# The last quarter of a late modulation moved beside the output projection, and a bias row added later

## The chip, the cores and the metric

The kernel runs on one core of a Trainium2 chip. The metric is the device time of a whole execution in microseconds (us), the median of several runs. Five engines work side by side, each through its own queue in order: PE multiplies matrices, DVE, ACT and POOL work element by element, and SP here only issues DMAs.

## The reference, cut to what matters

One block of a diffusion backbone over 1024 latent and 256 context tokens, 1024 wide. Six rows of modulation come from the condition vector c; the last three (the shift and scale of the MLP, `sh2` and `sc2`, and its gate `gt2`, called g2 below) and the gate `gt1` (g1) are wanted late.

```python
m = jax.nn.silu(cvec) @ w_ada + b_ada
sh1, sc1, gt1, sh2, sc2, gt2 = jnp.split(m[:, None, :], 6, axis=-1)
p_lat = modulate(rmsnorm(x, g_mix), sh1, sc1) @ w_in
p_ctx = modulate(rmsnorm(ctx, g_mix), csh1, csc1) @ w_in
y_lat = token_mixers(p_ctx, p_lat, ...)      # mLSTM, Mamba-2 SSD, RG-LRU
x = x + gt1 * (y_lat @ w_out)
x = x + gt2 * (jnp.square(jax.nn.relu(modulate(rmsnorm(x, g_mlp), sh2, sc2) @ w_mlp1 + b_mlp1)) @ w_mlp2 + b_mlp2)
return rmsnorm(x, g_final)
```

Everything is float32. A product is three matmuls on operands split into a high and a low part.

## The kernel before

The work runs in stages (times are those of the profiled run). Until 70 us the input is loaded and normalised, and the modulation's first third is computed on PE. From 70 to 156 us come the gates and the first feature tile of the RG-LRU, to 235 us its second tile and the q, k and v projections with their convolutions. To 365 us the mLSTM runs backward and forward with the projections x, c and b beside it, to 447 us the z projections and the backward part of the SSD. From 447 us the SSD sweep goes over eight latent chunks of 128 tokens, and the last projections fill PE between its steps; each chunk starts with products of a selector matrix, `SELB`, and needs the state of the chunk before. By 600 us w_out is split into high and low parts, and to 662 us the output projection runs: for each of eight token tiles two groups of 24 matmuls, the gate g1, the residual, the norm, and transposes into the MLP's operand (`x2_tile`). Then come the two MLP products, each by a seven-product scheme, the first of 56 products in eight blocks to about 976 us, the second to the end.

A list scheduler sets the order ahead of time: it places instructions on each engine's queue by a priority, and `at()` gives parts of the mixers due times from a table, `PLAN`, which fills the gaps of one part with another's work.

The late modulation is the product of the condition with columns 2048 to 6143 of `w_ada`, done on DVE: 64 jobs of 128 rows by 512 columns, eight to a row of the accumulator. A job loads 256 KB into a buffer and adds it, scaled per partition, to `ACCA` (line 727; the first of eight is line 725). After eight jobs `ada_flush` sums the accumulator over the partitions with four small matmuls against ones and adds the bias into `MODL`. The jobs are strewn in by `proj`: five ahead of each projection xr, q, k, v, x, c and b, until 64 are done. The buffer is a ring of six in the first stages, later a single tile. The last flush turns all of `MODL` into rows and stores them in `GD`, from where g1 and g2 are broadcast to all partitions (`bcast_row`).

Beside the output projection POOL multiplies `b_mlp2` by g2 into two tiles `WX` (line 1212) and adds them to the finished residual tiles 0 to 4 (line 1235) before these are stored to `X2D`. The first MLP product then carries side jobs on POOL between its products: tiles 5 to 7 of `X2D` are loaded, get b2*g2 added and are stored again (line 1483), and the 32 row tiles of `w_mlp2` are multiplied by g2 and stored (line 1485). The splits of the first MLP's operands run on ACT and DVE (line 1311), the sums and differences of its scheme on DVE (line 1339).

## Time and profile before

| | us |
|---|---|
| runs | 1299.17, 1303.20, 1304.24 |
| median | 1303.2 |
| profiled execution | 1300.48 |
| its span | 1298.8 |
| busy PE / PEld / DVE | 1228.0 / 964.4 / 979.9 |
| busy ACT / POOL | 564.8 / 285.1 |
| mean granted TensorE clock | 0.986 |

A busy share is an average over all stages. The views below cut it into stretches; in the timelines the time in brackets is how long the engine had been idle, and what it waited for. PEld is the loading of weights, which runs beside the matmuls.

### The profile page before, as it was taken

The numbers are of one execution on the slowest core, as the hardware profiler recorded it, in microseconds if no ns is written. First come the engines' busy times: TensorE is split into PE (matmuls) and PEld (weight loads), VectorE is DVE, ScalarE is ACT, GpSimd is POOL, SyncE is SP. The second block draws the span as 40 slices with busy tenths as digits, with TensorE's granted clock in tenths as the row PEclk, the third lists the DMA queues.
The fourth block names the chain that finished last, engine by engine and source line by source line (L and its number), as shares of the span: only waits on it lengthen the run. The fifth ranks groups of instructions, "written<-read, shape, count | busy, mean of one in ns | idle before, by whom it ended". The sixth has DMA issues, their size and how long they took to land.

```text
span 1298.8 us, 16517 instructions
## 1 busy us (share of the span) xinstructions
PE 1228.0 (95%) x6066; PEld 964.4 (74%) x6066; DVE 979.9 (75%) x1416; ACT 564.8 (43%) x891; POOL 285.1 (22%) x290
## 2 busy tenths in 40 slices
PE   4888898999999889999999999999999999999997
PEld 1566667788786667677888888888787888888886
DVE  3798977787774675677569876677668988989985
ACT  3546572343333334254466534553357433333432
POOL 2430212212322235213500254345200000000000
PEclk9899999999999999999999999999999999999999
DMA  9444402642325522145333589877679142330112
GB/s 314 155 134 143 130 17 82 183 131 70 125 63 165 169 75 74 57 147 170 116 112 130 175 296 323 290 258 277 243 255 365 75 149 111 128 132 1 56 58 98
DMA packets 122790, 196.48 MB, mean 151 GB/s; under 512 B 11126, under 2 KB 71892, under 8 KB 121172
## 3 DMA queue, kind: packets, MB, share of 16 engines
q1 hardware_dynamic: 122708, 195.42, 45.5%
q8 instruction: 48, 0.79, 0.3%
q14 instruction: 34, 0.28, 0.1%
HBM read 140.76 MB, written 54.63 MB: 150 GB/s over the span
## 4 chain that ended last, share of the span: by engine, by line
PE 56%; DVE 3%; DMA 2%; ACT 1%; issue 1%; POOL 1%; POOLq 0%; DVEq 0%; SPq 0%; ACTq 0%
PE pp L53 28%; PE pd L53 16%; PE psx L53 6%; PE psa L53 2%; PE psb L53 2%; PE psl L53 1%; PE pst L53 1%; DMA wx<-ZD 1%; DMA rw<-in_w_mlp_dram 1%; PE pst L1266 1%; DVE rw L1339 0%; DMA g1B<-GD 0%; POOL KV L1062 0%; POOL xp L1020 0%; DVE rbd L857 0%
## 5 line engine op out<-in xcount | busy, mean ns | idle before, releaser
L53 PE MATMUL pd<-xh,wht 128*128 128x512 f32 (+1 forms) x304 | 126.2, 418 | 3.2 <-DVE wx L1111 1.7
L53 PE MATMUL pd<-xh,wlt 128*128 128x512 f32 (+1 forms) x304 | 126.3, 417 | 1.7 <-POOL wlt L352 1.7
L53 PE MATMUL pd<-xl,wht 128*128 128x512 f32 (+1 forms) x304 | 123.2, 409 | 3.9 <-DVE xl L235 1.8
L1485 POOL TENSOR_TENSOR ax<-ax,g2B 128x1024 f32<-128x1024 f32 x32 | 84.6, 2647 | 92.4 <-DMA ax<-in_w_mlp_dram 92.4
L53 PE MATMUL pp<-ob,yb 128*128 128x512 f32 x324 | 97.6, 395 | 0.0
L352 POOL TENSOR_TENSOR wlt<-wraw,wht 128x512 fp32r<-128x512 f32 x40 | 58.2, 1456 | 177.6 <-ACT wht L351 143.6
L1339 DVE TENSOR_TENSOR rw<-rw 128x1024 f32<-128x1024 f32 (+1 forms) x33 | 64.8, 1965 | 32.0 <-DMA rw<-in_w_mlp_dram 19.1
L1684 POOL TENSOR_TENSOR ss<-ss,V 128x1 f32<-128x1 f32 x8 | 5.2, 644 | 355.9 <-DVE ss L1683 355.9
L53 PEld LDWEIGHTS pp<-ob,yb 128*128 128x128 f32 x324 | 60.7, 187 | 14.9
L53 PEld LDWEIGHTS pd<-xh,wht 128*128 128x128 f32 (+1 forms) x304 | 58.0, 191 | 17.9 <-DVE wx L1111 2.1
L53 PEld LDWEIGHTS pd<-xl,wht 128*128 128x128 f32 (+1 forms) x304 | 57.9, 190 | 16.1 <-DVE xl L235 4.9
L53 PEld LDWEIGHTS pd<-xh,wlt 128*128 128x128 f32 (+1 forms) x304 | 58.0, 191 | 14.1 <-POOL wlt L352 2.5
L351 ACT ACTIVATE wht<-wraw 128x512 fp32r<-128x512 f32 (+2 forms) x50 | 28.5, 581 | 67.0 <-PE pd L53 17.4
L53 PE MATMUL pp<-ob,wht 128*128 128x512 f32 x144 | 53.5, 395 | 0.0
L1310 ACT ACTIVATE ya<-rw 128x1024 fp32r<-128x1024 f32 x26 | 27.5, 1058 | 42.0 <-issue 14.2
L1400 ACT ACTIVATE pp<-pp,V 128x512 f32<-128x512 f32 x35 | 23.0, 656 | 50.9 <-DVE pp L1395 50.7
L53 PE MATMUL psx<-xc,wht 128*128 128x256 f32 (+1 forms) x192 | 42.8, 293 | 1.4 <-POOL xc L235 0.7
L53 PE MATMUL pp<-ya,wlt 128*128 128x512 f32 x124 | 43.0, 391 | 0.0
L53 PEld LDWEIGHTS psx<-xc,wht 128*128 128x128 f32 (+1 forms) x192 | 33.7, 188 | 8.1 <-POOL xc L235 1.2
L1311 DVE TENSOR_TENSOR ya<-rw,ya 128x1024 fp32r<-128x1024 f32 x18 | 24.9, 1388 | 13.2 <-ACT ya L1310 13.1
L53 PE MATMUL pp<-yb,wlt 128*128 128x512 f32 x88 | 34.3, 390 | 0.0
L53 PE MATMUL pd<-ya,wlt 128*128 128x512 f32 x88 | 34.2, 389 | 0.0
(838 smaller groups left out, 3461.4 us busy)
## 6 DMA issues: line engine op xcount, KB each, us to landing
ax<-in_w_mlp_dram SPq DMA_DIRECT2D x33, 512.0 KB, 6.2
rw<-in_w_mlp_dram SPq DMA_DIRECT2D x32, 512.0 KB, 5.5
W2S<-ax SPq DMA_DIRECT2D x32, 512.0 KB, 3.5
wraw<-in_w_in_dram SPq DMA_DIRECT2D x44, 256.0 KB, 2.9
radt<-in_w_ada_dram SPq DMA_DIRECT2D x40, 256.0 KB, 3.0
ada<-in_w_ada_dram SPq DMA_DIRECT2D x16, 512.0 KB, 5.5
HD<-wraw SPq DMA_DIRECT2D x16, 512.0 KB, 3.7
HD<-g1B SPq DMA_DIRECT2D x16, 512.0 KB, 3.3
```

What stands on the lines that cost most here:

```text
L53: return T.matmul(o, l, r, start=start, stop=stop)
L351: S.activation(out=ph, in_=pr, func=AF.Copy)
L352: (V if split or name[0:2] == "xr" else G).tensor_tensor(out=pl, in0=pr, in1=ph.bitcast(F32), op=ALU.subtract)
L1266: T.transpose(pt[:, k, :], xn[:, (4 * g + k) * P:(4 * g + k + 1) * P], ident)
L1310: S.activation(out=hi[:, c], in_=src[:, c], func=AF.Copy)
L1311: (e or V).tensor_tensor(out=lo[:, c], in0=src[:, c], in1=hi[:, c].bitcast(F32), op=ALU.subtract)
L1339: RS[2] = (e or V).tensor_tensor(out=q[o], in0=q[x0], in1=q[x1], op=op)
L1400: S.activation(out=ps, in_=ps, func=AF.Relu, bias=V2[:, 40 + f:41 + f])
L1485: G.tensor_tensor(out=u, in0=u, in1=g, op=ALU.mult)
L1684: G.tensor_tensor(out=rs, in0=ss[:, 1:2], in1=MHALF, op=ALU.pow)
```

## The change

The 64 jobs are split differently. Ahead of the projections there are fewer now: three for xr, q, k and v, four for x, c and b, which makes 48. After the SSD's features the sixth row is flushed, and the first 8 of the 32 rows of 128 in `MODL`, which hold g1, go to `GD`. The last 16 jobs, the two accumulator rows of g2, are issued in the output projection, four after each of the first four token tiles, with a ring of four buffers in `AXA` and an accumulator in `AX2`. With the fifth tile come the last flush, the second transposition and store, the broadcast of g2 and the products b2*g2. The additions of b2*g2 before the spill are gone: all eight tiles of `X2D` get them in the first MLP product, where 40 side jobs in place of 35 start two products sooner. The splits of that product's weights whose tile shares its place with `AXA` come later. `PLAN` is as it was.

```diff
--- before.py
+++ after.py
@@ -354,17 +354,19 @@
             ls.append(wl)
         return hs, ls
 
+    NADA = {"q": 3, "k": 3, "v": 3, "x": 4, "c": 4, "b": 4, "z": 0, "g": 0, "o": 0}
+
     def proj(name, col, segs, evac, gates=False):
         m = 48 if gates else P
         early = name.startswith("xr")
         if early:
-            ada_late(5)
+            ada_late(3)
         with (prio({"xr0": pxr0, "xr1": pxr1}[name]) if early else tc.high_priority()):
             if gates:
                 hs, ls = wsplit(name, ((0, C_IG, 16), (16, C_DT, 16)), 32, True)
             else:
-                if not early and not name.startswith("z"):
-                    ada_late(5)
+                if not early:
+                    ada_late(NADA[name[0]])
                 hs, ls = wsplit(name, ((0, col, P),), P, False)
         for grp in ([(0,), (1, 2)] if len(segs) == 3 else [(0,), (1,)]):
             ps = {}
@@ -699,32 +701,31 @@
     ada_pos = [0]
     GD = drp.tile([32, P], F32, name="GD")
 
-    def ada_flush(r):
-        pm = psx[:, 0:4]
+    ACC = [ACCA]
+
+    def ada_flush(r, pm):
         for i in range(4):
-            mm(pm[:, i:i + 1], ACCA[:, i * P:(i + 1) * P], ones[:, 0:1])
-        V.tensor_tensor(out=MODL[:, 4 * r:4 * r + 4], in0=pm, in1=V2[:, 4 * r:4 * r + 4], op=ALU.add)
-
-    def ada_late(n):
+            mm(pm[:, i:i + 1], ACC[0][:, i * P:(i + 1) * P], ones[:, 0:1])
+        V.tensor_tensor(out=MODL[:, 4 * r:4 * r + 4], in0=pm[:, 0:4], in1=V2[:, 4 * r:4 * r + 4], op=ALU.add)
+
+    def mod_rows(r0, n, pm, o):
+        T.transpose(pm[0:n, 0:P], MODL[:, r0:r0 + n], ident)
+        S.activation(out=o[0:n, 0:P], in_=pm[0:n, 0:P], func=AF.Copy)
+        SY.dma_start(out=GD[r0:r0 + n], in_=o[0:n, 0:P])
+
+    def ada_late(n, ring=None):
         for _ in range(n):
             i = ada_pos[0]
             ada_pos[0] += 1
             r, k = i // KT, i % KT
-            if k == 0 and 0 < r <= 8:
-                ada_flush(r - 1)
-                if r == 8:
-                    V.scalar_tensor_tensor(out=MODL[:, 16:24], in0=MODL[:, 16:24], scalar=1.0, in1=V2[:, 32:40], op0=ALU.add, op1=ALU.mult)
-                    T.transpose(psx[0:32, 0:P], MODL, ident)
-                    S.activation(out=WX[0][0:32, 0:P], in_=psx[0:32, 0:P], func=AF.Copy)
-                    SY.dma_start(out=GD, in_=WX[0][0:32, 0:P])
-            if r >= 8:
-                return
+            if k == 0 and r in (1, 2, 3, 4, 5, 7):
+                ada_flush(r - 1, ring.get([P, 4]) if ring else psx)
             t = radt.get([P, 512])
             SY.dma_start(out=t, in_=w_ada[k * P:(k + 1) * P, 2048 + 512 * r:2560 + 512 * r])
             if k == 0:
-                V.tensor_scalar(out=ACCA, in0=t, scalar1=SCL[:, k, 0:1], scalar2=None, op0=ALU.mult)
+                V.tensor_scalar(out=ACC[0], in0=t, scalar1=SCL[:, k, 0:1], scalar2=None, op0=ALU.mult)
             else:
-                V.scalar_tensor_tensor(out=ACCA, in0=t, scalar=SCL[:, k, 0:1], in1=ACCA, op0=ALU.mult, op1=ALU.add)
+                V.scalar_tensor_tensor(out=ACC[0], in0=t, scalar=SCL[:, k, 0:1], in1=ACC[0], op0=ALU.mult, op1=ALU.add)
 
     with ExitStack() as st:
         cp = st.enter_context(pool("cp"))
@@ -1135,6 +1136,9 @@
     with at(PLAN["mo"]):
         mlstm_out()
     ssd_features()
+    ada_flush(5, psx)
+    V.scalar_tensor_tensor(out=MODL[:, 16:24], in0=MODL[:, 16:24], scalar=1.0, in1=V2[:, 32:40], op0=ALU.add, op1=ALU.mult)
+    mod_rows(0, 8, psx, WX[0])
     z_spill()
     ssd_back()
     YC = [SAt[0], SAt[1]]
@@ -1200,16 +1204,14 @@
     X2L = [p2a.tile([P, KT, 512], F32R, tag="x0l", name="x0l")]
     g1B = p2a.tile([P, D], F32, name="g1B")
     g2B = p2a.tile([P, D], F32, name="g2B")
-    OPX = p2a.tile([P, 2048], F32R, tag="ax1", name="opx")
+    AXA = p2a.tile([P, 2048], F32, tag="ax1", name="axa")
     AX2 = p2a.tile([P, 1536], F32, name="ax2")
     p2x = ExitStack()
     p2b = p2x.enter_context(tc.tile_pool(name="p2b", bufs=1, reuse_waits="tile"))
     wo_prep(5, p2b.tile([P, D], F32R, name="woh5"), p2b.tile([P, D], F32R, name="wol5"))
-    for g, r in ((g1B, 0), (g2B, 24)):
-        bcast_row(g, GD[r:r + 8, :].rearrange("r q -> (r q)"))
-    for h in range(2):
-        bcast_row(WX[h], a["b_mlp2"][0, 512 * h:512 * h + 512])
-        G.tensor_tensor(out=WX[h], in0=WX[h], in1=g2B[:, 512 * h:512 * h + 512], op=ALU.mult)
+    bcast_row(g1B, GD[0:8, :].rearrange("r q -> (r q)"))
+    ACC[0] = AX2[:, 1024:1536]
+    radt = Sub([AXA[:, 512 * i:512 * i + 512] for i in range(4)])
     pW = Sub(pA.t + pB.t + pL.t + [psx] + PD[0][:2])
 
     pso = {}
@@ -1226,13 +1228,8 @@
 
     wo_mm((0, 0), (0, 1), (1, 0), (1, 1))
     XQ, X2T = [], {}
-    LATE = 5
 
     def x2_store(t):
-        if t < LATE:
-            for h in range(2):
-                o = X2T[t][:, 512 * h:512 * h + 512]
-                G.tensor_tensor(out=o, in0=o, in1=WX[h], op=ALU.add)
         SY.dma_start(out=X2D[t], in_=X2T[t])
 
     def x2_tile(t):
@@ -1282,6 +1279,15 @@
     for t in range(6):
         x2_tile(t)
         x2_store(t)
+        if t < 4:
+            ada_late(4, pT)
+        if t == 4:
+            ada_flush(7, pT.get([P, 4]))
+            mod_rows(24, 8, pT.get([P, P]), AXA)
+            bcast_row(g2B, GD[24:32, :].rearrange("r q -> (r q)"))
+            for h in range(2):
+                bcast_row(WX[h], a["b_mlp2"][0, 512 * h:512 * h + 512])
+                G.tensor_tensor(out=WX[h], in0=WX[h], in1=g2B[:, 512 * h:512 * h + 512], op=ALU.mult)
 
 
     wox.close()
@@ -1324,6 +1330,7 @@
     XIN = {1: "11", 2: "21", 6: "T2", 5: "T1", 7: "T3", 3: "22", 4: "T4"}
     AIN = {1: "11", 2: "12", 3: "12", 4: "22", 5: "21", 6: "11", 7: "21"}
     rq = {n: RW[:, 1024 * j:1024 * j + 1024] for j, n in enumerate(("11", "12", "21", "22"))}
+    OPX = p2a.tile([P, 2048], F32R, tag="ax1", name="opx")
     R1 = [WHT, WLT]
     ops1 = []
     U1 = AX2[:, 0:1024]
@@ -1470,7 +1477,7 @@
     W2S = drp.tile([4096, D], F32, name="W2S")
     AX1 = p2a.tile([P, 2048], F32, tag="ax1", name="ax1")
     w2b = [AX1[:, 0:1024], AX1[:, 1024:2048], AX2[:, 0:1024]]
-    jobs = [(X2D[t], X2D[t], None) for t in range(LATE, 8)] + [(w2[r * P:(r + 1) * P, :], W2S[r * P:(r + 1) * P, :], g2B) for r in range(32)]
+    jobs = [(X2D[t], X2D[t], None) for t in range(8)] + [(w2[r * P:(r + 1) * P, :], W2S[r * P:(r + 1) * P, :], g2B) for r in range(32)]
 
     def side_job(r):
         if 0 <= r - 2 < len(jobs):
@@ -1494,7 +1501,7 @@
         if n > 8:
             op1(n + 4)
         with tc.issue_after(ld[0].ins):
-            side_job(n - 14)
+            side_job(n - 12)
 
 
     ORDER = (1, 2, 5, 6, 3, 7, 4)
```

On DVE, at the exponentials of the first RG-LRU feature (lines 669 to 674 before), the queue before reads as follows; `wx` is the accumulator and `radt` the ring of loaded tiles:

```order
L727 SCALAR_TENSOR_TENSOR wx_94<-radt_612,SCL,wx_94 128x512
L669 SCALAR_TENSOR_TENSOR GR<-cp_622,GR 128x1282
L727 SCALAR_TENSOR_TENSOR wx_94<-radt_613,SCL,wx_94 128x512
L670 SCALAR_TENSOR_TENSOR cp_617<-cp_617,cp_623 128x1282
L727 SCALAR_TENSOR_TENSOR wx_94<-radt_614,SCL,wx_94 128x512
L727 SCALAR_TENSOR_TENSOR wx_94<-radt_615,SCL,wx_94 128x512
L670 SCALAR_TENSOR_TENSOR cp_620<-cp_620,cp_623 128x1282
L706 TENSOR_TENSOR MODL<-psx,V_78 128x4
L725 TENSOR_SCALAR wx_94<-radt_610,SCL 128x512
L727 SCALAR_TENSOR_TENSOR wx_94<-radt_611,SCL,wx_94 128x512
L669 SCALAR_TENSOR_TENSOR cp_619<-cp_622,cp_619 128x1282
```

And in the changed kernel (its lines are one to three higher there):

```order
L728 SCALAR_TENSOR_TENSOR wx_94<-radt_612,SCL,wx_94 128x512
L672 SCALAR_TENSOR_TENSOR cp_617<-cp_617,cp_623 128x1282
L728 SCALAR_TENSOR_TENSOR wx_94<-radt_613,SCL,wx_94 128x512
L671 SCALAR_TENSOR_TENSOR GR<-cp_622,GR 128x1282
L672 SCALAR_TENSOR_TENSOR cp_620<-cp_620,cp_623 128x1282
L671 SCALAR_TENSOR_TENSOR cp_619<-cp_622,cp_619 128x1282
L676 TENSOR_TENSOR cp_617<-GR,cp_617 128x1282
L676 TENSOR_TENSOR cp_620<-cp_619,cp_620 128x1282
L680 SCALAR_TENSOR_TENSOR GR<-cp_618,cp_617 128x256
L680 SCALAR_TENSOR_TENSOR cp_619<-cp_621,cp_620 128x256
```

The feature's own steps now follow each other; the jobs that stood between them are ahead of them or gone.

On PE, ahead of the fifth chunk of the sweep, the queue before has the chunk's preparation (a transposition of `TB` and the score products of `cT` and `bT`) amid the filling projection matmuls (`pd`):

```order
L53 MATMUL pd_66<-xl_86,wht 128x512
L53 MATMUL pd_66<-xh_85,wlt 128x512
L53 MATMUL pst_561<-ones,wx_94 128x1
L849 MATMUL pst_562<-ident,TB 128x128
L53 MATMUL pst_561<-ones,wx_94 128x1 x3
L53 MATMUL psa_563<-cT,bT 128x128
L53 MATMUL psb_564<-cT,bT 128x128
L53 MATMUL pd_65<-xh_87,wht 128x512
L53 MATMUL pd_65<-xl_88,wht 128x512
```

In the changed kernel that preparation stands further ahead, and the filling matmuls run up to the chunk's own products:

```order
L53 MATMUL pd_66<-xl_86,wht 128x512
L53 MATMUL pd_66<-xh_85,wlt 128x512
L53 MATMUL pst_561<-ones,wx_94 128x1 x4
L53 MATMUL psl_565<-rbd_1677,rcol_1681 128x512
L53 MATMUL psl_565<-MK_591,identR 128x512
L53 MATMUL psx<-rbd_1677,rcol_1682 128x512
```

Between the fourth chunk's first `SELB` product and the fifth's there are 78 filling matmuls before and 110 now.

On SP, at the end of the output projection, before:

```order
L1246 DMA x_6_5040<-in_x_dram 128x1024
L1236 DMA X2D<-x_5_4928 128x1024
L1246 DMA x_7_5130<-in_x_dram 128x1024
L1336 DMA rw<-in_w_mlp_dram 128x4x256 x4
L1236 DMA X2D<-x_6_5040 128x1024
L1236 DMA X2D<-x_7_5130 128x1024
```

And now:

```order
L724 DMA axa<-in_w_ada_dram 128x512 x3
L1243 DMA x_6_5034<-in_x_dram 128x1024
L1233 DMA X2D<-x_5_4921 128x1024
L1243 DMA x_7_5124<-in_x_dram 128x1024
L714 DMA GD<-axa 8x128
L1158 DMA g2B<-GD 128x1024
L1343 DMA rw<-in_w_mlp_dram 128x4x256 x4
L1233 DMA X2D<-x_6_5034 128x1024
L1233 DMA X2D<-x_7_5124 128x1024
```

The last jobs' loads and the two transfers through `GD` stand ahead of the first weights of the MLP (`rw`).

## Rows read from the trace of the kernel before

**Rows 1.** The page's list of busy times: us, share of the span, instructions.

```profile
PE 1228.0 (95%) x6066; PEld 964.4 (74%) x6066; DVE 979.9 (75%) x1416; ACT 564.8 (43%) x891; POOL 285.1 (22%) x290
```

**Rows 2.** Windows by stage: length, busy us of PE, PEld, DVE, ACT, POOL.

```profile
70.00:156.00 86.00, 75.92 (x363) 57.05 (x363) 80.84 (x129) 44.47 (x65) 18.93 (x28) 0.98 0.47 142
156.00:235.00 79.00, 71.74 (x336) 55.57 (x338) 55.49 (x49) 42.07 (x59) 18.54 (x36) 0.96 0.23 65
235.00:365.00 130.00, 126.11 (x712) 102.73 (x711) 105.51 (x258) 48.29 (x91) 29.95 (x63) 0.97 0.41 122
447.00:545.00 98.00, 90.40 (x698) 65.70 (x696) 66.44 (x126) 33.84 (x63) 40.61 (x32) 1.00 0.24 66
600.00:662.00 62.00, 62.00 (x290) 50.69 (x289) 34.27 (x59) 26.02 (x71) 25.45 (x23) 1.00 0.35 117
```

**Rows 3.** Windows of 50 us, same columns.

```profile
600.00:650.00 50.00, 50.00 (x234) 40.91 (x233) 28.00 (x48) 20.18 (x56) 24.90 (x22) 1.00 0.39 130
...
900.00:950.00 50.00, 48.05 (x204) 38.99 (x203) 34.04 (x32) 23.06 (x34) 13.71 (x6) 0.97 0.61 218
```

**Rows 4.** Windows, DVE's work of line 727, then of line 725, alone.

```profile
70.00:156.00 86.00, 23.95 (x28) 0.98 0.47 142
...
70.00:156.00 86.00, 1.92 (x4) 0.98 0.47 142
```

**Rows 5.** Timeline of DVE: start us, us, engine, line, operation, count, idle before.

```profile
128.80 1.50 DVE L669 SCALAR_TENSOR_TENSOR GR<-cp,GR 128x1282 f32<-128x1282 f32 x1 [2.13 <-ACT cp L668]
...
152.68 2.81 DVE L682 TENSOR_TENSOR cp<-GR,cp 128x1024 f32<-128x1024 f32 x1
...
171.25 1.50 DVE L669 SCALAR_TENSOR_TENSOR GR<-cp,GR 128x1282 f32<-128x1282 f32 x1 [7.01 <-ACT cp L668]
```

**Rows 6.** Waits of PE, 156 to 235 us: total us, times, longest.

```profile
PE pst L53 <- ACT GR L661: 4.0, 1, 4.0
```

**Rows 7.** The chain that ended last: start us, us, what.

```profile
482.44 11.56 PE pd L53 x50
...
597.60 0.76 DVE xn L1259
...
644.50 5.57 PE psb L53 x24
```

**Rows 8.** Timeline of PE around one flush.

```profile
361.89 0.95 PE L53 MATMUL psx<-ones,wx 128*128 128x1 f32 x8
362.70 0.49 PE L53 MATMUL pd<-xl,wht 128*128 128x512 f32 x1
```

**Rows 9.** Line 727: ns min/median/max; then who waited for it.

```profile
L727 DVE SCALAR_TENSOR_TENSOR wx<-radt,SCL,wx x35: 721/745/1786, 80.0 to 225.8; 128x512 f32<-128x512 f32 x35
...
  PE psx L53: 4.0, 2
```

**Rows 10.** The page's DMA issues: count, KB each, us to landing.

```profile
radt<-in_w_ada_dram SPq DMA_DIRECT2D x40, 256.0 KB, 3.0
```

**Rows 11.** Timeline of SP: the first weights of the MLP.

```profile
659.33 2.03 SPq L1336 DMA_DIRECT2D rw<-in_w_mlp_dram  x4
```

**Rows 12.** Lines 1235 and 1485 on POOL: ns min/median/max.

```profile
L1235 POOL TENSOR_TENSOR x<-x,wx x10: 1280/1286/2279, 598.6 to 635.3; 128x512 f32<-128x512 f32 x10
...
L1485 POOL TENSOR_TENSOR ax<-ax,g2B x32: 2386/2408/3483, 759.7 to 931.0; 128x1024 f32<-128x1024 f32 x32
```

**Rows 13.** Timeline of DVE, the last block of the first MLP product.

```profile
921.45 1.32 DVE L1339 TENSOR_TENSOR rw<-rw 128x1024 f32<-128x1024 f32 x1 [6.57 <-DMA rw<-in_w_mlp_dram]
...
931.14 3.35 DVE L1339 TENSOR_TENSOR rw<-rw 128x1024 f32<-128x1024 f32 x1
```

**Rows 14.** Waits of PE, 662 to 960 us.

```profile
PE pp L53 <- DVE uu L1391: 2.0, 1, 2.0
```

**Rows 15.** Window between the sweep's fourth and fifth chunk, columns as in rows 2.

```profile
477.70:503.00 25.30, 24.93 (x156) 19.62 (x155) 13.88 (x24) 8.85 (x17) 11.78 (x9) 1.00 0.19 53
```

## The prediction, made before the changed kernel was run

> **What bounds the kernel now.** I read the page's list of busy times first: PE is busy for 1228.0 of 1298.8 us [rows 1], so nearly all there is to win lies in the 70 us in which it is not. Then I cut the span by stage [rows 2], because an average hides where those 70 us are. From 600 us on PE is full: 62.00 of 62 us in the output projection, and in the first MLP product the one dent is 1.95 us at 900 to 950 [rows 2, 3]. The idle time that an edit can reach is in the mixers. Of these the stage from 70 to 156 us (gate mathematics and the first RG-LRU feature) stands out: DVE is busy there for 80.84 of 86 us and PE for 75.92, so PE has 10.1 us idle and DVE 5.2. In every other mixer stage DVE stands well below PE: 55.49 of 79, 105.51 of 130, 66.44 of 98 [rows 2].
>
> Third, I looked at who fills DVE in that stage. The accumulations of the late modulation (line 727, and line 725 for the first of each eight) take 23.95 us in 28 and 1.92 us in 4: 32 of the 64 jobs, 25.9 us, stand in the one stage where DVE is short [rows 4]. DVE's timeline shows its queue without a gap over 2.13 us until the feature's last sum at 152.68 [rows 5].
>
> **The change part by part.** The profiled run took 1300.48 us, 1.7 of them outside its span; it is 2.7 us below the median of 1303.2. The sum is made on 1300.48, and 2.7 added at the end.
>
> *Sixteen jobs fewer in the mixers.* By the new order all sixteen disappear ahead of the first RG-LRU feature's end: 32 jobs stood there, now 16. From there to the sweep 32 stand in both. So the relief falls into the DVE-bound stage alone. Half of its jobs is 14 x 0.855 us (23.95 / 28) + 2 x 0.48 = 12.9 us off DVE [rows 4]. Not all of it can reach the end. Late next is ACT, whose exponentials and squares (line 668) already make DVE wait 2.13 us; the second feature, with none of these jobs in between, shows how long that wait is without cover: 7.01 us [rows 5]. I therefore take off 7.0 - 2.1 = 4.9 us and have 12.9 - 4.9 = **-8.0 us**, which also stays within PE's 10.1 us idle. Bounds: -12.9 if ACT keeps up, 0 if ACT's or PE's own chain sets the pace (ACT makes PE wait 4.0 us in the next stage, line 661 [rows 6]). A loss is excluded, as nothing is added to this stage.
>
> *Matmuls that change places.* With other work ready at other times, the scheduler puts 63 projection matmuls behind the sweep's first chunk that stood ahead of it (between the first chunk and the last 159 before, 226 now). Fifty of them run in 11.56 us [rows 7], 0.231 each: 14.6 us. They leave a stage in which PE is 97% busy (126.11 of 130) and enter one where it is 92% busy (90.40 of 98) [rows 2]. A matmul that moves from one full stretch to another changes nothing, so I take **0**, with bounds of -7.6 (the sweep's idle PE time takes half of them for nothing) and +14.6 (the stages ahead end no sooner, and the sweep is longer by all of them).
>
> *Flushes.* Two of the eight flushes, which turn an accumulated row by four small products, leave the mixers for the output projection, and a second transposition joins them. A flush holds PE for 0.81 us, from 361.89 to 362.70 [rows 8]. In the saturated stage that is 2 x 0.81 + 0.2 = 1.8 us more, in the mixers 1.6 less; I take **+0.2** (up to +1.8, if the mixers do not return it).
>
> *Sixteen jobs in the output projection.* DVE gets 14 x 0.745 (the median of line 727 [rows 9]) + 2 x 0.48 = 11.4 us. It is busy for 34.27 of 62 there; 45.7 of 62 fit beside PE's 62.00 [rows 2]. What hides them is PE's queue of 24-matmul groups of 5.57 us each [rows 7], issued two token tiles ahead. Ahead of the first normalised tile (597.60 [rows 7]) five jobs, 3.7 us, now stand where three splits of a weight operand stood, which go behind it. I take **0**: PE holds issued groups at that point. The cost without that cover is 3.7, and -1 is possible, since the splits are the longer work. Sixteen loads of 256 KB go through SP's queue and into four buffers; behind a load that waits for its buffer stand the next x tile and the spills of finished tiles. A load lands in 3.0 us [rows 10], so four buffers can bring a job every 0.75 us, and one every 3.9 us (62 / 16) is wanted. One new wait has work behind it: the store of the second part of the modulation waits for the last flush, and behind it on SP stand the broadcast of g2 and the first weights of the MLP. Those left at 659.33 [rows 11]; the last flush stands behind the group of 644.50 that ends at 650.07 [rows 7], nine us sooner. So 0 again, at most +3.
>
> *POOL.* Ten additions of b2*g2 (line 1235, 1.286 us each) leave the output projection; nobody waited for them, so 0 [rows 12]. Five more pairs of load and store, with ten additions, go to the head of the MLP's side jobs. These start two slots sooner and end three later, so three multiplications of 2.41 us (line 1485 [rows 12]) now run beside the last block's operands. What that does is visible already: line 1339 takes 1.32 us while POOL rests and 3.35 while it multiplies [rows 13], and PE waits 2.0 us just there for line 1391 [rows 14]. Three times 2.03 is +6.1 at worst; 0 if the longer instructions stay hidden; I take **+1.0**, near the 2.0 that the place costs now.
>
> The Trainium skill ("GPSIMD Engine Reference", section "8. Key points") has a rule for this: GpSimd shares its SBUF interfaces with VectorE, and they contend when a VectorE instruction has two inputs in SBUF. The 1.32 against 3.35 us agrees.
>
> Sum: -8.0 + 0 + 0.2 + 0 + 1.0 = -6.8 us: 1293.7 on the profiled run, **1296 us** on the median's basis.
>
> **The rivals.**
>
> *The sweep takes the moved matmuls for nothing.* For it: PE idles 7.6 of 98 us there [rows 2], and a matmul that fills a wait is free. Against: between the fourth chunk and the fifth, where 32 of the 63 go, PE is already busy for 24.93 of 25.30 us [rows 15]. Time: -6.8 - 7.6 = -14.4, 1289. The Trainium skill ("Perfetto Trace Analysis", section "Identifying the Most-Contended Engine") calls matmul busy time a poor measure of PE's headroom and weight-load time a good one. Weight loads take 65.70 of 98 us in the sweep and 40.91 of 50 in a full window [rows 2, 3], so by that rule all 63 would fit, and the time would be 1282.
>
> *Nothing comes through.* ACT or PE's own chain, not DVE, sets the end of the first RG-LRU feature. For it: ACT ended DVE's longest gaps [rows 5] and PE's longest wait [rows 6]. Against: PE itself waits 4.0 us in two waits for line 727 [rows 9]. Time: 0 + 1.2, 1304.
>
> *The other side: the sweep is lengthened.* The sweep is a chain, since each chunk needs the last one's state, and PE works in order: what fills the space between two chunks must be done before the next chunk's products. Between the fourth chunk and the fifth PE has 0.4 us idle [rows 15], and 32 more matmuls there are 7.4 us; with the other 31 unabsorbed too it is 14.6, while the sweep starts only the 8 us sooner that DVE gives. Against: they are work that PE must do anyway, so the sweep should start sooner by more. Time: -8 + 14.6 + 1.2 = +7.8, 1311. It decides from the point where the stretch from the sweep's first chunk to the output projection grows by over 8 us.
>
> *The MLP's last block waits.* The three late multiplications hold up its operands: +6.1 in place of +1, with half of the first term, so -4 + 0.2 + 6.1, 1305. For it: the present 2.0 us. Against: this is PE's only wait from 662 to 960 us [rows 14].
>
> *The moved jobs are not hidden.* Beside POOL's work on SBUF a job of line 727 can take 1786 ns instead of 745 [rows 9]; if all sixteen did, 16 x 1.04 = 16.7 us would bring DVE to 62.4 of 62 us, and PE would wait. By the skill's rule above these jobs, with two inputs in SBUF, are of the kind that meets POOL. Against: with its additions gone POOL works there less than its 25.45 us now [rows 2]. Time: the bounds of 3.7 and 3 on top of -6.8, 1303.
>
> **How the numbers follow.** Forecast 0.38 (its own range 1291 to 1301), the sweep for nothing 0.16, nothing 0.22, the sweep lengthened 0.14, the last block 0.06, not hidden 0.04. The range runs from 1284, between the first rival's two prices, to 1309, short of the third rival's full price; that leaves out about 2 in 10. Under 0.5%, 6.5 us, a measurement here cannot tell a change from none. Faster (below 1296.7): two thirds of the forecast, the first rival and a little of the second, 0.45. Slower (above 1309.7): most of the third, with parts of the last two and of what I do not see, 0.18. Same: 0.37.
>
> **What would show it.** The sum that ends the first RG-LRU feature should come about 8 us before 152.68, with DVE below 90% in that stage and longer gaps at the exponentials. The sweep should begin some 20 us sooner and be some 14 us longer. The output projection should show PE full and DVE near 46 of 62 us. The last multiplication on POOL should run beside the last block. If the first feature ends as late as now, the first term is wrong; if the sweep grows by more than it starts sooner less 8 us, the second is; if PE waits in the output projection, the fourth.

## The result and the profile after

The changed kernel takes 1314.42 us (median of 1313.34 to 1319.67), the kernel before, run again beside it, 1302.31. The ratio is 1.0112, with a 95% interval of 1.0077 to 1.0147: 10 to 19 us slower. The forecast was 1296, and its range ended at 1309. The profiled execution's span is 1312.4 us, 13.6 longer than before.

The same views, in the order of the rows ahead of the prediction. The page's list of busy times [rows 1]:

```profile
PE 1230.4 (94%) x6067; PEld 963.9 (73%) x6067; DVE 981.0 (75%) x1416; ACT 567.8 (43%) x894; POOL 293.2 (22%) x290
```

The windows by stage [rows 2], with the sweep's stretch from its fourth chunk to its fifth as the last row [rows 15]:

```profile
70.00:156.00 86.00, 73.76 (x345) 54.67 (x343) 67.08 (x110) 52.12 (x72) 15.04 (x27) 0.98 0.32 98
447.00:545.00 98.00, 90.62 (x646) 67.26 (x644) 55.21 (x105) 31.10 (x58) 37.30 (x29) 1.00 0.24 68
600.00:662.00 62.00, 62.00 (x299) 51.00 (x298) 42.55 (x70) 28.26 (x73) 17.61 (x16) 1.00 0.50 171
...
465.70:501.70 36.00, 32.87 (x187) 25.34 (x185) 14.71 (x27) 11.20 (x21) 12.64 (x11) 1.00 0.31 88
```

In the first stage DVE has fallen from 80.84 to 67.08 us, as the moved jobs should make it. PE has not risen: 73.76 where it was 75.92. The output projection is full, with DVE at 42.55. Between the fourth chunk and the fifth stand 36.0 us where there were 25.3. DVE's timeline of the first feature and the end of the second [rows 5]:

```profile
134.22 1.53 DVE L671 SCALAR_TENSOR_TENSOR cp<-cp,cp 128x1282 f32<-128x1282 f32 x1 [2.19 <-ACT cp L670]
...
146.46 1.93 DVE L684 TENSOR_TENSOR cp<-GR,cp 128x1024 f32<-128x1024 f32 x1
155.41 0.82 DVE L403 TENSOR_SCALAR qT<-cp,V 128x1024 f32<-128x1024 f32 x1 [7.01 <-ACT cp L424]
```

The feature's last sum starts 6.2 us sooner, 146.46 against 152.68, and the wait for ACT at the exponentials is as long as before, 2.19 us. So the stage itself did nearly what was forecast of it. But the relief ends there: DVE's next piece, the convolution of q, starts at 155.41 us, after 7.01 us of waiting for ACT, and in the kernel before it started at the same time:

```profile
155.35 0.79 DVE L401 TENSOR_SCALAR qT<-cp,V 128x1024 f32<-128x1024 f32 x1
```

Two places then lose time. The first lies before the sweep. These are PE's waits from 365 to 447 us, the windows around the longest of them, and the last accumulations in the mixers by DVE (line 728 is line 727 of before [rows 9]):

```profile
PE psa L53 <- DVE bT L433: 3.8, 1, 3.8
PE psx L53 <- DVE wx L728: 1.7, 1, 1.7
```

```profile
365.00:380.00 15.00, 15.00 (x77) 12.74 (x76) 12.42 (x16) 6.27 (x10) 4.50 (x7) 1.00 0.48 144
380.00:395.00 15.00, 9.27 (x48) 6.70 (x46) 8.49 (x8) 7.52 (x11) 3.73 (x2) 0.87 0.41 118
395.00:410.00 15.00, 12.99 (x48) 8.08 (x49) 6.57 (x16) 3.69 (x9) 0.00 (x0) 0.56 0.51 153
```

```profile
L728 DVE SCALAR_TENSOR_TENSOR wx<-wx,SCL,wx x21: 736/746/1754, 228.4 to 394.6; 128x512 f32<-128x512 f32 x21
```

With three or four jobs ahead of each projection in place of five, the 48th job comes at 394.6 us, where the 64th came at 360.9. The last jobs now stand in DVE's queue amid the convolution of `bT`, for which PE waits. DVE's and PE's timelines there, in the changed kernel:

```profile
379.75 0.75 DVE L728 SCALAR_TENSOR_TENSOR wx<-wx,SCL,wx 128x512 f32<-128x512 f32 x1 [1.74 <-DMA wx<-in_w_ada_dram]
...
383.47 0.75 DVE L728 SCALAR_TENSOR_TENSOR wx<-wx,SCL,wx 128x512 f32<-128x512 f32 x1
386.26 1.50 DVE L433 SCALAR_TENSOR_TENSOR bT<-xq,bT 128x1282 f32<-128x1282 f32 x1 [2.04 <-ACT xq L432]
```

```profile
387.81 0.58 PE L53 MATMUL psa<-cT,bT 64*128 64x128 f32 x1 [3.81 <-DVE bT L433]
```

and in the kernel before:

```profile
392.22 1.50 DVE L431 SCALAR_TENSOR_TENSOR bT<-xq,bT 128x1282 f32<-128x1282 f32 x1 [0.83 <-ACT xq L430]
```

```profile
402.89 0.37 PE L53 MATMUL psa<-cT,bT 64*128 64x128 f32 x1
```

Two jobs and the load that one of them waits for take 3.2 us of DVE's time ahead of the last step of `bT` (0.75 + 1.74 + 0.75), and the flush behind the last job makes PE wait another 1.7 us. But the late jobs are not the whole cause. `bT` is ready 6.0 us sooner than before, and PE comes to its product 18.9 us sooner, at 384.0 us where it was 402.9: some of the projection matmuls that kept it busy until then have moved behind, into the sweep. PE was idle for 5.7 of 15 us, and in the 15 us that followed its clock was 0.56 of full speed. The second place is the first MLP product: PE reaches the last tile's transposes 2.3 us later than before (675.96 against 673.71 in its timeline) and the end 13.6 us later. PE's waits from 690 to 960 us [rows 14], and a window at the longest:

```profile
PE pd L53 <- DVE uu L1398: 3.3, 1, 3.3
PE pd L53 <- ACT wraw L1408: 1.6, 1, 1.6
PE psx L53 <- ACT wraw L1408: 1.6, 1, 1.6
```

```profile
855.00:870.00 15.00, 11.67 (x40) 8.94 (x39) 13.86 (x12) 3.33 (x5) 9.51 (x4) 0.77 0.81 280
```

One wait of 2.0 us has become several, 7.8 us in all, and behind the longest the clock fell to 0.77; behind those of 1.6 us it stayed at 1.00. What the longest waits for is late weights: an addition that stands in DVE's queue behind the sums of the weights, and DVE itself waits for these to land. (Three of DVE's steps from there to PE's wait take 3.0 to 3.3 us beside POOL's multiplications, in place of 1.2; in the kernel before two take 2.8 and 3.3.)

```profile
849.78 1.23 DVE L1346 TENSOR_TENSOR rw<-rw 128x1024 f32<-128x1024 f32 x1 [7.49 <-DMA rw<-in_w_mlp_dram]
```

SP's timeline shows why; in the changed kernel, with a row's first number the time of issue and its second how long it held SP:

```profile
751.32 0.82 SPq L1343 DMA_DIRECT2D rw<-in_w_mlp_dram  x1
752.26 8.09 SPq L1484 DMA_DIRECT2D X2D<-ax  x2
760.76 0.38 SPq L1343 DMA_DIRECT2D rw<-in_w_mlp_dram  x1
...
773.69 7.41 SPq L1484 DMA_DIRECT2D X2D<-ax  x3
...
799.77 0.38 SPq L1343 DMA_DIRECT2D rw<-in_w_mlp_dram  x1
```

and in the kernel before, the last weights of the same two blocks:

```profile
749.90 0.38 SPq L1336 DMA_DIRECT2D rw<-in_w_mlp_dram  x1
...
790.36 1.07 SPq L1336 DMA_DIRECT2D rw<-in_w_mlp_dram  x1
```

The stores of the spilled tiles wait for POOL's additions, which wait for the tiles' loads, and the weights (`rw`) stand behind them. They are those of the fourth and the fifth of the eight blocks (the expectations below call the fourth the third). The last of each leave 9 to 11 us later, and those of the later blocks 10 to 13, while PE starts the fifth block only 2.7 us later than before.

### The profile page after: what moved, and what is told of

Read it like the earlier page. It is cut to its first block, busy times and chain, and to the rows that moved or that the text cites. A ratio compares the mean times of both kernels' runs of the same rounds, so it can differ in the third digit from the quotient of the medians.

```text
span 1312.4 us, 16522 instructions
## 1 busy us (share of the span) xinstructions
PE 1230.4 (94%) x6067; PEld 963.9 (73%) x6067; DVE 981.0 (75%) x1416; ACT 567.8 (43%) x894; POOL 293.2 (22%) x290
## 5 line engine op out<-in xcount | busy, mean ns | idle before, releaser
L53 PE MATMUL pd<-xh,wht 128*128 128x512 f32 (+1 forms) x304 | 123.4, 409 | 4.0 <-DVE wx L1112 2.9
L53 PE MATMUL pd<-xh,wlt 128*128 128x512 f32 (+1 forms) x304 | 123.4, 406 | 1.7 <-POOL wlt L352 1.7
L53 PEld LDWEIGHTS pd<-xh,wht 128*128 128x128 f32 (+1 forms) x304 | 56.5, 186 | 18.9 <-DVE wx L1112 4.0
L1490 POOL TENSOR_TENSOR ax<-ax,wx 128x512 f32<-128x512 f32 x16 | 27.6, 1757 | 79.2 <-PE pd L53 58.4
```

What stands on the lines that cost most here:

```text
L53: return T.matmul(o, l, r, start=start, stop=stop)
L1490: G.tensor_tensor(out=u[:, 512 * h:512 * h + 512], in0=u[:, 512 * h:512 * h + 512], in1=WX[h], op=ALU.add)
```

## The experiments

Ratios are to the kernel before on the same chip, with their 95% interval; 0.001 is 1.3 us.

**The halves apart.** The MLP side alone, on the kernel before:

```diff
-    LATE = 5
+    LATE = 0
-            side_job(n - 14)
+            side_job(n - 12)
```

> The kernel before with the second half of the change alone: all 64 jobs stay in the mixers, all eight tiles get b2*g2 in the first MLP product, whose 40 side jobs start two products sooner. Theory A (the loss is the side jobs' queue: the weights of the blocks leave SP some 10 us late behind five more pairs of load and store): about 1313, with the mixers, the sweep and the last tile's transposes (673.7) as before and all of the loss between there and 1000 us. Theory B (the loss is in the mixers and the sweep, by the 63 matmuls that moved): about 1302, no change.

1310.68 us, 1.0082 (1.0052 to 1.0112): +10.7 us, with the mixers' order as before. SP's timeline has the stall of the changed kernel:

```profile
747.07 8.02 SPq L1477 DMA_DIRECT2D X2D<-ax  x2
755.19 0.38 SPq L1336 DMA_DIRECT2D rw<-in_w_mlp_dram  x1
```

The moved jobs alone, from the changed kernel:

```diff
-    jobs = [(X2D[t], X2D[t], None) for t in range(8)] + [...]
+    jobs = [(X2D[t], X2D[t], None) for t in range(5, 8)] + [...]
-            side_job(n - 12)
+            side_job(n - 14)
```

> The changed kernel with its MLP side as before: three pairs and 32 multiplications from product 14 on; the additions of b2*g2 to tiles 0 to 4 are left out, so its time is that of the moved jobs alone. PE's order is that of the changed kernel to the last row. Theory A: about 1304 (the last tile's transposes came 2.3 us later in the changed kernel, and nothing behind that is lost). Theory B: about 1313, as the changed kernel.

1309.12 us, 1.0049 (1.0014 to 1.0084): +6.4 us. Neither theory had both halves lose. Together they make 17, within the interval of the whole change. So the 2.3 us of the one pair of profiles above are too few for the moved jobs.

**Is DVE's work in the mixers worth anything?**

```diff
-V.scalar_tensor_tensor(out=ACCA, in0=t, ..., in1=ACCA, ...)
+V.scalar_tensor_tensor(out=ACCA[:, 0:8], in0=t[:, 0:8], ..., in1=ACCA[:, 0:8], ...)
```

> The kernel before with 56 of the 64 accumulations cut from 512 columns to 8 (most of the modulation is left out): loads, flushes and matmuls stay, DVE loses some 47 us of work, 23 of them in the stage from 70 to 156 us. Theory P (PE fills what DVE makes it wait with matmuls that it must do anyway, so only PE's own idle time can be won): at most 4 us faster, the waits for line 727, so 1298 to 1302. Theory D (the forecast's first term: DVE's work in that stage sets the end): twice the forecast's relief, 13 us or more, 1289 or less.

1303.3 us, 1.0013 (0.9986 to 1.0040). A job of 8 columns still takes 226 ns, so DVE lost 29 us in all (951.2 where it was 979.9) and not 47; the stage from 70 to 156 us:

```profile
70.00:156.00 86.00, 76.35 (x366) 57.39 (x366) 65.19 (x130) 52.82 (x75) 16.51 (x27) 0.98 0.47 147
```

That is 15.7 us less than the 80.84 of [rows 2], more than the change takes, and PE's 76.35 is the 75.92 of before. The feature's last sum starts at 142.10 us, 10.6 sooner, and DVE then waits 10.15 us for ACT. No time came back: theory P; a gain of over 1.8 us lies outside the interval.

**Why the moved jobs lose.** In the same kernel as the moved jobs alone, the mixers' 48 jobs put where the first 48 stood, five ahead of each projection:

```diff
-NADA = {"q": 3, "k": 3, "v": 3, "x": 4, "c": 4, "b": 4, ...}
+NADA = {"q": 5, "k": 5, "v": 5, "x": 5, "c": 5, "b": 5, ...}
-            ada_late(3)
+            ada_late(5)
+            if ring is None and ada_pos[0] >= 48:
+                return
```

> The moved jobs alone (MLP side as before, additions to tiles 0 to 4 left out), but the 48 jobs of the mixers stay where the first 48 stood: five ahead of each projection, none ahead of the last. In the changed kernel the last of them ended at 394.6 us in place of 360.9, amid the convolution for which PE then waited 3.8 us, with the clock at 0.56 of full speed behind it. Theory L (that place makes the moved jobs' loss): the wait is gone and 1.6 us of flushes in the output projection stay, 1300 to 1304. Theory O (any move of them costs, by the order or in the output projection): 1306 to 1310.

1303.92 us, 1.0009 (0.9988 to 1.0029): in theory L's range. Its last job in the mixers is at 260.2 us, and the windows around the place of the wait:

```profile
380.00:395.00 15.00, 15.00 (x72) 12.27 (x71) 7.60 (x8) 5.00 (x9) 3.38 (x3) 1.00 0.34 94
395.00:410.00 15.00, 14.93 (x82) 11.16 (x80) 3.60 (x6) 6.51 (x12) 2.58 (x2) 1.00 0.50 139
```

This edit takes back more than the late place. It puts 32 jobs into the stage from 70 to 156 us again (DVE is busy for 79.28 us there), and with them the matmuls ahead of the sweep. So it shows that the new arrangement of the mixers loses the time, and not how much of that is the late jobs and how much the matmuls that moved.

The counterpart keeps the late place and leaves out the 16 jobs of the output projection (its MLP side is as in the moved jobs alone):

```diff
-        if t < 4:
-            ada_late(4, pT)
-            ada_flush(7, pT.get([P, 4]))
+            V.tensor_copy(out=MODL[:, 24:32], in_=V2[:, 24:32])
```

> The mixers of the changed kernel (three or four jobs ahead of each projection, 48 in all) with the 16 jobs of the output projection left out, so without the product that makes g2, which is the bias alone, and the MLP side as before. Theory L (the late place of the mixers' last jobs makes PE wait and its clock fall): the loss of the moved jobs alone less the flush's 0.8 us in the output projection, 1305 to 1309. Theory O (the 16 jobs in the output projection cost): as the kernel before, 1300 to 1304.

1306.71 us, 1.0032 (1.0006 to 1.0059): slower by itself, as theory L has it, though the interval reaches near theory O's bound. The wait for `bT` is there (3.7 us), and so is the clock of 0.61 from 395 to 410 us. One by one these intervals overlap, but the profiles of all runs agree: PE starts the first MLP product at 665.0 to 672.3 us in the eight kernels with the changed mixers, at 658.9 to 664.3 in the eight with the mixers of before, and at 659.6 to 663.9 in the four with the mended place.

**What in the MLP side loses.** First the changed kernel with the start two products later (its `side_job(n - 12)` made `n - 14`):

> The changed kernel with the 40 side jobs starting at product 14 as before, so ending at product 55. Theory A1 (the number of side jobs costs): as slow as the changed kernel, 1312 to 1318. Theory A2 (the early start costs, since the first pairs then stand ahead of the second and third block's weights): most of it comes back, 1304 to 1308.

1312.76 us, 1.0086 (1.0051 to 1.0121), between the theories' bounds; it does not settle them. Each alone on the kernel before, the early start with 35 jobs and then eight pairs with the old start:

> The kernel before with its 35 side jobs starting two products sooner. Theory A2 (the early start costs: the first pairs stand ahead of the third block's weights): 1306 to 1311. Theory A1 (the number of pairs costs): 1300 to 1303.

1305.66 us, 1.0018 (1.0001 to 1.0036).

> The kernel before with eight pairs in place of three (no additions in the output projection) and the start where it was, so that the side jobs end five products later. Theory A1: 1308 to 1313. Theory A2: 1301 to 1305, since the third block's weights leave as before.

1305.55 us, 1.0032 (1.0015 to 1.0049). Each costs some: 2.3 and 4.2 us, where both together cost 10.7 (the intervals, 0.1 to 4.7, 2.0 to 6.4 and 6.8 to 14.6, leave open whether that is more than the sum). Neither theory is right alone, because the two lose in different places. In the changed kernel PE waits for 6.2 us from 690 to 942 us and for 3.4 from 945 to 1000, where the kernel before has 2.0 and 0.7. The early start alone has 5.5 and 0.2, the eight pairs alone 3.6 and 5.9, and the changed kernel with the later start 0.5 and 7.6; these are the 7.6:

```profile
PE pd L53 <- ACT g1B L1408: 2.5, 2, 1.8
PE pp L53 <- ACT wraw L1408: 2.1, 1, 2.1
PE pd L53 <- ACT wraw L1408: 1.6, 1, 1.6
PE pp L53 <- ACT g1B L1408: 1.4, 2, 0.7
```

So the later start trades the late weights for waits from the last block to the start of the second product.

The pairs without their additions, and the additions without their transfers, both on the changed kernel:

```diff
-                    G.tensor_tensor(out=u[...], in0=u[...], in1=WX[h], op=ALU.add)
+                pass
```

> The changed kernel with the eight pairs of load and store of the spilled tiles kept and their sixteen additions of b2*g2 on POOL left out. Theory S (what costs is SP's queue: stores and loads that wait for a buffer stand ahead of the next block's weights): the transfers alone hold the queue nearly as long, 1310 to 1315. Theory G (what costs is POOL's additions, by their time or by colliding with DVE): without them as the moved jobs alone, 1305 to 1309.

1307.87 us, 1.0047 (1.0024 to 1.0070): in theory G's range, and the moved jobs' loss alone. The transfers alone do hold SP, as the stores wait for their loads to land:

```profile
749.57 5.92 SPq L1484 DMA_DIRECT2D X2D<-ax  x2
755.59 0.38 SPq L1343 DMA_DIRECT2D rw<-in_w_mlp_dram  x1
```

That is 5.92 us in place of 8.09, and the weights behind leave 5.2 us sooner than in the changed kernel. It is soon enough: PE's waits from 690 to 942 us fall from 6.2 us to 0.2. Theory S was wrong on the time that the transfers alone cost, and theory G leaves open by what way the additions cost.

```diff
-            SY.dma_start(out=u, in_=src)
+            if g is not None:
+                SY.dma_start(out=u, in_=src)
-        if 0 <= r - 2 < len(jobs):
+        if 8 <= r - 2 < len(jobs):
```

> The changed kernel with the eight pairs' transfers left out and sixteen additions of the same size on POOL kept in their slots (on the bias tiles, so the tiles in memory stay without b2*g2). Theory S: as the moved jobs alone, 1305 to 1309, with the third block's last weights leaving within 5 us of the kernel before. Theory G: as the changed kernel, 1312 to 1317.

1311.0 us, 1.0058 (1.0031 to 1.0086), between the two expectations: by its ratio +7.6 us, near the moved jobs alone, by its median not. Its additions, without transfers to wait for, crowd into the first blocks (twelve of the sixteen in one row from 706 to 728 us), so it is no clean test.

The queue itself gives the better test. The side jobs' loads and stores are issued by POOL, and SP keeps the weights:

```diff
-            SY.dma_start(out=jobs[r - 2][1], in_=w2b[(r - 2) % 3])
+            G.dma_start(out=jobs[r - 2][1], in_=w2b[(r - 2) % 3])
-            SY.dma_start(out=u, in_=src)
+            G.dma_start(out=u, in_=src)
```

On the kernel before, on the changed kernel, and on the changed kernel with the jobs' place mended:

> The kernel before with the loads and stores of its 35 side jobs issued by POOL in place of SP. Theory S (SP's queue holds back the weights): the wait at 935 us and the slow clock behind it go, 1297 to 1301 where the kernel before has 1303. Theory T (the DMA engines or POOL's time bound the weights and the side jobs): 1303 to 1308, the side jobs later by what POOL spends on issuing.

1304.9 us, 1.0022 (0.9991 to 1.0053): no gain there; theory T's price, or none. PE's wait at 935 us and the slow clock behind it did go, as theory S had it (20.00 of 20 us busy from 930 to 950, at 1.00), but the time did not.

> The changed kernel with the loads and stores of its 40 side jobs issued by POOL. Theory S: the blocks' weights leave as early against PE as in the kernel before and what stays is the moved jobs' 6 us, 1306 to 1310. Theory T: as the changed kernel or slower, 1313 to 1320.

1306.8 us, 1.0029 (1.0005 to 1.0053): 11 us of the 15 are back, theory S, with POOL's additions all there. (Issuing on POOL also spreads the side jobs, whose last multiplication ends at 973 us in place of 959, so the queue is not all that differs.) SP's timeline no longer has the stall:

```profile
752.77 0.37 SPq L1343 DMA_DIRECT2D rw<-in_w_mlp_dram  x1
754.81 0.34 SPq L1410 DMA_DIRECT2D HD<-g1B  x1
755.24 3.36 SPq L1343 DMA_DIRECT2D rw<-in_w_mlp_dram  x2
```

> The full change with the jobs' place mended (five ahead of each projection) and the side jobs issued by POOL. Theory S: 1301 to 1305, level with the kernel before. Theory T: 1311 to 1316.

1300.6 us, 0.9987 (0.9961 to 1.0013), just below theory S's range. With both losses mended the change is level with the kernel before, and no better by any margin that can be measured.

The same mended place with the MLP side as changed, on SP, and with the later start, shows that the halves are apart:

> The full change (eight pairs, start at product 12) with the 48 jobs of the mixers five ahead of each projection. If the halves add up: 1.2 us of the mended move and 10.7 of the MLP side, 1312 to 1316 where the kernel before has 1302. If they do not (the MLP side only costs beside the late sweep): 1304 to 1309.

1311.57 us, 1.0072 (1.0047 to 1.0097): +9.4, 0.4 us short of the range for halves that add up and above the other. With this run the place is mended in three pairs of runs (the moved jobs alone, the whole change on SP, the whole change on POOL's queue), and it gives back 5.2, 5.2 and 5.5 us.

> As the run before it with the start at product 14. If the early start and the number of pairs cost more together than apart: 1.2 + 4.2, so 1306 to 1309, and 4 us or more less than with the start at product 12. If they simply add up: within 3 us of the run with the start at product 12.

1308.36 us, 1.0043 (1.0022 to 1.0065): +5.6, as expected if the early start and the number cost more together; but 3.8 us less than the run before it lies between the two cases, so that stays open.

**Other places for b2*g2.** In the second product, on POOL, as the accumulators are loaded, with no pairs (first on the kernel before, then on the changed one):

```diff
+    for i, h in ((0, 0), (0, 1), (1, 0)):
+        d = half(acc[2 * i + h], 512)
+        G.tensor_tensor(out=d, in0=d, in1=WX[h].unsqueeze(1).broadcast_to([P, 4, 512]), op=ALU.add)
```

> The kernel before (64 jobs in the mixers) with no additions of b2*g2 in the output projection and no pairs in the first MLP product: the second product's accumulators get b2*g2 on POOL, idle there, as they are loaded (four additions of 128 x 2048). Theory S: the side jobs' queue is three slots shorter, the wait at 935 us and the slower clock behind it go: 1296 to 1300 where the kernel before has 1301. Theory G: POOL's wide additions hold up DVE at the start of the second product: 1301 to 1306.

1315.61 us, 1.0091 (1.0056 to 1.0125): theory G's way, but 11.9 us where its range allowed 5.

> The changed kernel's moved jobs with b2*g2 added in the second MLP product as in the run before, and 32 side jobs from product 14. Theory S: the whole loss of the MLP part is gone and what stays is that of the moved jobs, 1303 to 1308. Theory G: as the changed kernel less little, 1309 or more.

1319.72 us, 1.0135 (1.0108 to 1.0162): 17.6 us, which is the moved jobs' 6.4 and some 11 again. POOL's and DVE's timelines of the first of the two:

```profile
976.21 15.91 POOL L1626 TENSOR_TENSOR acc<-acc,wx 128x2048 f32<-128x2048 f32 x3 [46.03 <-ACT pp L1400]
```

```profile
976.54 5.66 DVE L1339 TENSOR_TENSOR qxh<-qxl,qxh 128x1024 f32<-128x1024 f32 x1
982.12 0.69 DVE L1395 TENSOR_TENSOR pp<-pp,uu 128x512 f32<-128x512 f32 x1
982.72 5.03 DVE L1339 TENSOR_TENSOR qxh<-qxh 128x1024 f32<-128x1024 f32 x1
```

Last, all eight tiles before their spill on the kernel before (`LATE = 8`), so with no pair at all:

> The kernel before with b2*g2 added to all eight tiles on POOL ahead of their spill, so without any pair in the first MLP product: 32 side jobs from product 14. Theory S (the side jobs' queue on SP sets when the last blocks' weights leave): three slots fewer, the wait at 935 us and the slower clock behind it go, 1296 to 1300 where the kernel before has 1301 to 1302. Theory G (POOL's additions collide with DVE): six more additions stand beside DVE's differences at 650 to 690 us, no gain or 2 to 4 us lost, 1302 to 1306.

1302.97 us, 1.0002 (0.9979 to 1.0024). PE's wait at 935 us is gone, and two of about 1 us each have come at 689 and 715 us. Both effects are there, and the time shows neither; that they cancel is likely and not shown.

## Why the prediction was wrong, step by step

*Sixteen jobs fewer in the mixers, -8.0 us.* This step failed: it was worth nothing that the runs can measure. Its stage came out nearly as foretold (DVE at 78% there, the first feature's end 6.2 us sooner), but the end of a stage that DVE bounds is not time of the kernel. PE does not stand still while DVE is behind: the scheduler lets it run projection matmuls that must be run anyway, so when DVE is quicker they only move behind. What can be won is PE's own idle time, and that does not shrink: 10.1 us in the stage before, 12.2 in the changed kernel, 9.7 when 15.7 us of DVE's work went. The argument did name PE's idle time as a limit, and then took it for a gain. "Nothing comes through" was the right rival on this step. It gave ACT's or PE's own chain as the reason. The filler is PE's, and ACT has a part that no run separates: PE's waits for ACT at the gates (line 661 of before) are 4.5 us from 70 to 235 us before and 6.6 in the changed kernel. The 4.9 us that the sum took off for a longer wait at the exponentials rest on a reading that did not hold: that wait is 2.19 us, and not 7.0.

*"From there to the sweep 32 stand in both."* True by number and wrong by place: fewer jobs ahead of each projection push the later ones back, to 394.6 us, onto a convolution that PE waits for. The bounds for this step said that a loss was excluded. The runs price the moved jobs alone at 6.4 us, of which 1.2 remain when the place is mended.

*Matmuls that change places, 0.* Half right. The windows from 70 us to the sweep's first chunk, and from there to the first matmul of w_out, before and after:

```profile
70.00:447.38 377.38, 353.40 (x1822) 274.23 (x1823) 289.88 (x534) 165.49 (x271) 84.10 (x145) 0.97 0.40 119
447.38:559.30 111.92, 102.67 (x778) 75.46 (x777) 74.19 (x143) 41.56 (x77) 42.62 (x33) 0.98 0.27 77
```

```profile
70.00:436.14 366.14, 336.25 (x1744) 259.27 (x1741) 274.04 (x512) 165.23 (x267) 84.92 (x141) 0.97 0.36 107
436.14:562.55 126.41, 117.12 (x840) 86.93 (x839) 76.95 (x144) 43.10 (x80) 46.22 (x36) 0.99 0.27 78
```

In the sweep the 0 was right: it is 14.5 us longer, and all of that is work, with PE idle for 9.3 us in both. Ahead of the sweep it was not: PE is idle for 29.9 us there in place of 24.0, so the sweep starts only 11.2 us sooner. What a matmul covered in its old place counts as well as the stretch that it joins. The third rival had this picture, a sweep that grows by more than it starts sooner, and its point, a stretch longer by over 8 us, was passed. That its +7.8 is near the 6.4 of the moved jobs is in part luck: it counts on 8 us from DVE, and it lays the loss to the sweep's own chain, where none is seen. The mended kernel does not make this trade (its sweep takes 113.8 us), so the price of the late jobs and that of the moved matmuls stay together.

*Flushes, +0.2, up to +1.8.* From the first tile's transposes to the last's PE takes 1.6 us more in its timeline, near the upper bound, as if the mixers returned nothing. *The output projection, 0:* right; PE is full there.

*POOL and the side jobs, +1.0.* Mis-sized: 10.7 us alone. The step counted POOL's three later multiplications and their collisions with DVE, to +6.1 at worst, and for the five more pairs of transfers it named no cost. SP's queue was read in the output projection, but not where the pairs are. The runs showed two costs in its place: weights that leave SP late from the fourth block on, and waits from the last block to the start of the second product, 3.4 us where there were 0.7. The rival of the last block's wait had the second alone.

## What to carry to other kernels

Where PE is kept busy by filler work of its own, read the gain of a relieved engine from PE's idle time and not from that engine's stage: a stage's bound can be lifted with nothing to show for it. When work is thinned out, follow its last piece as well as its number, and ask what the filler that moves with it had covered. And here a store that waited for an engine held everything behind it on its queue: where that holds back weights, give the transfers that wait another queue (on the kernel before, where it held back little, this gained nothing), and count each pair that is added.

## What the runs showed of the hardware

A wait can cost PE more than its length. In the changed kernel PE was idle for 5.7 of the 15 us from 380 to 395, and its granted clock was 0.56 of full speed in the 15 us that followed, nearly down to the 1.2 GHz level of the two (1.2 and 2.4 GHz). PE was busy for 13.0 of these 15 us; at full speed their work would have taken some 5.7 us less (0.44 x 13.0, an estimate). From 395 to 410 us the clock was 0.50 to 0.61 in all eight kernels that have this wait, and 1.00 in the other twelve. Not every wait has this price: behind single waits of 1.6 us in the first MLP product, as at 916 us in the changed kernel, the clock stayed at 1.00.

DVE's additions and subtractions of 128x1024 with both inputs in SBUF took 5.66 and 5.03 us beside POOL's additions of 5.3 us each, and 1.21 to 1.23 while POOL rested; the addition of a PSUM tile between them took its usual 0.69. The Trainium skill ("GPSIMD Engine Reference", section "8. Key points") says that the two engines contend for their shared SBUF interfaces where a VectorE instruction has two inputs in SBUF; this trace agrees, and shows the size: 3.8 and 4.4 us longer beside instructions of 5.3 us.
